# Streaming encoder layer on one core: the instruction order taken from a timeline simulation in place of the scheduler's usual machine model

## Chip, cores and metric

One NeuronCore of a Trainium2 chip runs the whole program in one launch. The metric is the device time of one execution in microseconds (us); lower is better. Engines are called PE (TensorE; PEld are its weight loads), DVE (VectorE), ACT (ScalarE), POOL (GpSimd) and SP (SyncE, which issues nearly all DMA transfers).

## The reference

One layer of a hybrid encoder is applied to two groups of rows that share all weights: 512 prompt rows and 64 sample rows of width 1024, in float32. Cut to what matters:

```
xn   = rmsnorm(x);  proj = xn @ w_in                      # 1024 x 3592
oa   = rmsnorm(gated_delta_rule(silu(conv(proj[q,k,v])))) * silu(z)   # 4 heads of 128
ob   = rmsnorm(softmax(q1 k1) v - lam * softmax(q2 k2) v)             # 4 heads of 128
h    = x + [oa, ob] @ w_out
h    = h + softmax(rmsnorm(h) @ w_mem_q  mem_k) mem_v @ w_mem_o       # 4 heads of 256
h    = h + relu(rmsnorm(h) @ w_ff1)**2 @ w_ff2                        # 1024 x 4096 x 1024
y    = rmsnorm(h)
```

The gated delta rule runs over blocks; within a block it needs the inverse of a triangular matrix, and from block to block it carries a 128 x 128 state for each head. The memory's keys and values (256 rows) are projected from a memory input for the prompt and read from a cache for the sample. Keys, values, states and convolution rows are outputs as well.

## The kernel before, in words

Rows and weights stay in float32, but the large products are made in three matmuls: each operand is split into a high part (a rounded copy, made on ACT) and a low part (the difference, made on DVE), and high x high, high x low and low x high are added up in PSUM. `weights` (L165) loads eight 128 x 128 blocks of a weight matrix into a `raw` tile (three buffers) and `split_weights` (L155) splits it into `wh` and `wl` (two buffers each). `project` (L169) multiplies it with all 576 columns in two halves, on one of three `pr` banks of PSUM, and an `evac` function carries the result away. `mm` (L106) and `tr` (L111) record every matmul and every transpose, so all of PE's rows in the profile bear L107 or L113; the tile's name tells which product it is (`pr` projections, `g` and `gs` small products of the delta rule and the attention, `ba` transposes and sums, later also products of the feed-forward part).

The stages follow each other in the code like this, though the engines overlap them:

- start (L365 to L429): rows are loaded, normed and turned, and the first three blocks of `w_in` are projected. This stage stands in `in_order()` (L52), which ties each engine's instructions to the order in which they are written.
- the rest of the q, k, v projections with the convolution (L440 to L463), about 35 to 105 us in the profile.
- the gated delta rule: `gdn_prep` (L653) makes, for each of four prompt chunks of 128 rows and one sample chunk, the gates and the triangular inverse, which it doubles level by level (five levels, L755 to L773, each a transpose and a product, a copy to SBUF, a second product, and a subtraction on DVE); `gdn_scan` (L811) then carries the state from chunk to chunk. Its square roots are powers on POOL (`rpow`, L207). The preparation of the next chunk, the scan of this one and the projections of z (`project_z`, L640) are independent and can be mixed.
- differential attention: `diff_project` (L946) makes q, k, v of a head, `diff_head` (L996) its scores, softmax and output for five row tiles.
- memory keys and values (L1080 to L1115), the output projection, memory attention (L1190 to L1249), with their projections.
- the feed-forward part: `ff1_pair` (L1380) makes two row blocks of the first product by seven products of sums of quarters, and `weights2`/`project` make the second product of the group before.
- the tail: last block, final norm, transposes back, stores.

What decides the order. The code is written as straight Python; every instruction is recorded with its tiles, and the order of each engine's queue is made when the `TileContext` closes. A list scheduler then steps a model of the machine. Each recorded instruction has a priority, the place where it stands in the code. Whenever an engine of the model can take an instruction, the scheduler gives it, among those whose inputs the model has finished and whose tile has a free buffer, the one with the highest priority. The buffer of a tile is chosen at the same time. The result is a fixed queue for every engine, SP and its transfers included, with semaphore waits between them. On the chip each queue runs in that order, whatever the real durations are. The scheduler's usual model is a core simulator that prices each instruction for its engine.

The code bends this order in four ways: `in_order()` (L52) for the start; `tc.high_priority()` around the splits of weights (L160, L1313, L1368), so that they come ahead of other ready work on ACT and DVE; `tc.keep_in_program_order` for single transfers, sums and transposes, most of them in the tail (`pin=True`); and `tc.issue_after(...)` (L467, L475, L599, L920, L940, L1561), which keeps early-ready work behind a named instruction of the same engine. These are edges that any order must keep.

Compiler passes after the scheduler put in the semaphore waits and the loads of ACT's function tables (Silu and Exp lie in different tables).

## Time and profile before

| | |
|---|---|
| runs | 987.23 us median of 3 (987.15 to 987.32) |
| the profiled execution | 987.2 us, of which the span from the first to the last instruction is 985.5 us |
| granted PE clock, mean | 0.997 |
| read from HBM, written | 79.93 MB, 9.75 MB |

The profile is one execution with every instruction's start and end on its engine. A row of instructions gives the line of the code, the engine, the operation, the tile written and the tiles read, the shape, the count, then busy time in us, the mean in ns, the idle time of the engine just before, and after an arrow the instruction that ended that idle time. A row of a timeline gives start and length in us. Ends of matmuls are modelled: the matmuls overlap in a pipeline, so that the busy time of PE is the time with at least one in it.

The chain of work that ended last, followed back from the end, runs over PE for 83% of the span, DVE for 4%, "issue" for 3%, and POOL, DMA and ACT for 2% each.

### The profile page before, as it was taken

The numbers are of one execution on the slowest core, as the hardware profiler recorded it, in microseconds if no ns is written. First come the engines' busy times: TensorE is split into PE (matmuls) and PEld (weight loads), VectorE is DVE, ScalarE is ACT, GpSimd is POOL, SyncE is SP. The second block draws the span as 40 slices with busy tenths as digits, with TensorE's granted clock in tenths as the row PEclk, the third lists the DMA queues.
The fourth block names the chain that finished last, engine by engine and source line by source line (L and its number), as shares of the span: only waits on it lengthen the run. The fifth ranks groups of instructions, "written<-read, shape, count | busy, mean of one in ns | idle before, by whom it ended". The sixth has DMA issues, their size and how long they took to land.

```text
span 985.5 us, 16923 instructions
## 1 busy us (share of the span) xinstructions
PE 968.5 (98%) x6403; PEld 891.2 (90%) x6403; DVE 699.7 (71%) x1570; ACT 530.1 (54%) x1194; POOL 58.8 (6%) x127
## 2 busy tenths in 40 slices
PE   9999999999999999999999999999999999999996
PEld 7989899898888878999999999999999999999996
DVE  6666787877676676666557977657867779978674
ACT  7545575344656665444445657665544445555444
POOL 3341011101000000000000000000000000000000
PEclk9999999999999999999999999999999999999998
DMA  7432340103222647333111414222222223223202
GB/s 212 129 119 65 90 138 23 43 23 103 81 68 68 203 131 227 95 94 99 44 44 58 127 54 127 86 86 86 86 87 86 86 86 86 86 86 86 65 23 96
DMA packets 121714, 90.75 MB, mean 92 GB/s; under 512 B 5564, under 2 KB 112206, under 8 KB 121122
## 3 DMA queue, kind: packets, MB, share of 16 engines
q1 hardware_dynamic: 121266, 89.03, 30.9%
q8 instruction: 50, 0.82, 0.3%
q10 hardware_dynamic: 368, 0.66, 0.2%
q14 instruction: 30, 0.25, 0.1%
HBM read 79.93 MB, written 9.75 MB: 91 GB/s over the span
## 4 chain that ended last, share of the span: by engine, by line
PE 83%; DVE 4%; issue 3%; POOL 2%; DMA 2%; ACT 2%; POOLq 0%; ACTq 0%; SPq 0%; DVEq 0%
PE pr L107 51%; PE g L107 12%; PE ba L107 10%; PE gs L107 6%; PE ba L113 3%; PE g L113 1%; POOL tg L208 1%; DMA r<-in_w_ff_dram 1%; DVE p L457 1%; DVE wl L162 0%; DMA grow<-gdram 0%; DMA raw<-in_w_ff_dram 0%; POOL X L607 0%; POOL X L608 0%; DVE on L809 0%
## 5 line engine op out<-in xcount | busy, mean ns | idle before, releaser
L107 PE MATMUL pr<-u,wh 128*128 128x320 f32 (+2 forms) x1240 | 328.7, 343 | 1.3 <-DVE p L323 1.2
L107 PEld LDWEIGHTS pr<-u,wh 128*128 128x128 f32 x1240 | 212.3, 188 | 18.0 <-DVE p L323 1.8
L107 PE MATMUL pr<-u,wl 128*128 128x256 f32 (+1 forms) x816 | 226.7, 302 | 0.0
L107 PEld LDWEIGHTS pr<-u,wl 128*128 128x128 f32 x816 | 149.9, 189 | 2.7 <-DVE wl L388 0.2
L162 DVE TENSOR_TENSOR wl<-raw,wh 128x1024 fp32r<-128x1024 f32 x65 | 79.4, 1223 | 41.3 <-ACT wh L161 41.0
L161 ACT CAST wh<-raw 128x1024 fp32r<-128x1024 f32 x65 | 68.1, 1048 | 65.7 <-PE pr L107 50.5
L107 PE MATMUL pr<-u,w2h 128*128 128x320 f32 (+1 forms) x384 | 98.5, 340 | 0.0
L1369 ACT CAST w2h<-r 128x512 fp32r<-128x512 f32 x56 | 34.7, 620 | 87.9 <-PE pr L107 85.3
L107 PE MATMUL pr<-f,w2h 128*128 128x320 f32 (+1 forms) x288 | 74.3, 340 | 0.1
L107 PEld LDWEIGHTS pr<-u,w2h 128*128 128x128 f32 x384 | 65.0, 188 | 4.5 <-ACT u L1452 0.3
L107 PE MATMUL pr<-u,w2l 128*128 128x256 f32 (+1 forms) x256 | 65.1, 295 | 0.0
L1454 DVE TENSOR_TENSOR u<-u,pr 128x256 f32<-128x256 f32 x96 | 42.3, 448 | 16.9 <-PE pr L107 16.2
L107 PE MATMUL ba<-u,wl 128*128 128x288 f32 x360 | 53.0, 296 | 0.4 <-ACT keep L1405 0.4
L107 PEld LDWEIGHTS pr<-f,w2h 128*128 128x128 f32 x288 | 48.7, 188 | 4.0 <-issue 1.1
L107 PEld LDWEIGHTS ba<-u,wl 128*128 128x128 f32 x360 | 49.2, 188 | 1.2 <-ACT keep L1405 1.1
L107 PE MATMUL pr<-f,w2l 128*128 128x256 f32 (+1 forms) x192 | 48.8, 295 | 0.0
L107 PEld LDWEIGHTS pr<-u,w2l 128*128 128x128 f32 x256 | 46.9, 188 | 1.5
L208 POOL TENSOR_TENSOR tiny<-tiny,nhalf 128x1 f32<-128x1 f32 (+4 forms) x10 | 8.7, 870 | 631.6 <-DVE tiny L1522 529.8
L1370 DVE TENSOR_TENSOR w2l<-r,w2h 128x512 fp32r<-128x512 f32 x56 | 38.5, 688 | 10.7 <-ACT w2h L1369 10.4
L107 PE MATMUL pr<-wh,u 128*128 128x512 f32 x128 | 41.4, 401 | 0.0
L1414 ACT ACTIVATE c<-c 128x288 f32<-128x288 f32 x48 | 20.6, 443 | 29.5 <-DVE c L1413 29.5
L107 PEld LDWEIGHTS pr<-f,w2l 128*128 128x128 f32 x192 | 35.2, 188 | 1.2
(514 smaller groups left out, 2025.1 us busy)
## 6 DMA issues: line engine op xcount, KB each, us to landing
raw<-in_w_ff_dram SPq DMA_DIRECT2D x36, 512.0 KB
raw<-in_w_in_dram SPq DMA_DIRECT2D x28, 512.0 KB
r<-in_w_ff_dram SPq DMA_DIRECT2D x56, 256.0 KB
raw<-in_w_mem_k_dram SPq DMA_DIRECT2D x8, 512.0 KB
raw<-in_w_mem_v_dram SPq DMA_DIRECT2D x8, 512.0 KB
raw<-in_w_out_dram SPq DMA_DIRECT2D x8, 512.0 KB
raw<-in_w_mem_q_dram SPq DMA_DIRECT2D x8, 512.0 KB
raw<-in_w_mem_o_dram SPq DMA_DIRECT2D x8, 512.0 KB
```

What stands on the lines that cost most here:

```text
L107: i = nc.tensor.matmul(out, lhsT, rhs, start=start, stop=stop, skip_group_check=skip_group_check)
L113: i = nc.tensor.transpose(out, in_, ident[:n, :n])
L161: A.copy(wh, raw)
L162: V.tensor_tensor(wl, raw, wh.bitcast(F32), ALU.subtract)
L208: G.tensor_tensor(out, in_, bc(nhalf[: in_.shape[0], 0:1], list(in_.shape)), ALU.pow)
L457: V.scalar_tensor_tensor(yv[:, :n], cb[:, i : i + n], cwt[:, m, i : i + 1], yv[:, :n], ALU.mult, ALU.add)
L1369: A.copy(wh, src)
L1370: V.tensor_tensor(wl, src, wh.bitcast(F32), ALU.subtract)
L1414: A.activation(c, c, AF.Relu)
L1454: V.tensor_tensor(am, am, b, ALU.add)
```

## The change

The scheduler steps another model of the machine: a simulation of the occupancy over time of each device in the core (sequencers, engines, PE's weight loader and array, DMA queues), with time for decoding, for waiting in an engine's queue, for the landing of a matmul's result and for semaphores to spread. It takes every function table of ACT as loaded. The list scheduler, the priorities, the tiles with their numbers of buffers, the edges that the code adds and all instructions recorded are those of before; which instruction is found ready at which moment, and so the order of each queue and the choice among buffers, comes from the other model.

```diff
@@ -1616,7 +1616,7 @@
-    with _tile.TileContext(nc) as tc:
+    with _tile.TileContext(nc, schedule_with_timeline_sim=True) as tc:
         hybrid_layer_kernel(tc, *args)
     r = _run(nc, [arrays], core_ids=[0])
```

## The prediction

> **What bounds the kernel now.** I read the page's head first, then the table by stretches of the span, then the waits of TensorE, and last the order of work around the longest of those waits. The page's head:
>
> ```profile
> span 985.5 us, 16923 instructions
> PE 968.5 (98%) x6403; PEld 891.2 (90%) x6403; DVE 699.7 (71%) x1570; ACT 530.1 (54%) x1194; POOL 58.8 (6%) x127
> ```
>
> The profiled execution took 987.2 us: a span of 985.5 and 1.7 around it. The median of the runs shown is 987.23, so a sum made against this execution holds for the runs. TensorE (PE) is busy for 968.5 us, so 985.5 - 968.5 = 17.0 us of it are visibly idle. Where those 17 us lie is in the stretches (columns: length, then busy time and instructions of PE, PEld, DVE, ACT and POOL, granted clock, DMA share, GB/s):
>
> ```profile
> 0.00:20.00 20.00, 18.35 (x97) 14.06 (x98) 10.93 (x14) 15.00 (x26) 9.11 (x23) 1.00 0.69 200
> 20.00:100.00 80.00, 78.72 (x514) 73.55 (x513) 53.74 (x94) 43.06 (x86) 25.36 (x75) 1.00 0.39 112
> 100.00:200.00 100.00, 97.44 (x726) 89.99 (x725) 81.45 (x228) 55.70 (x118) 11.87 (x14) 1.00 0.26 72
> 200.00:300.00 100.00, 98.20 (x666) 85.70 (x665) 71.39 (x221) 51.77 (x156) 5.79 (x9) 1.00 0.27 73
> 300.00:372.00 72.00, 71.03 (x402) 57.80 (x401) 49.13 (x133) 45.67 (x131) 3.95 (x5) 1.00 0.44 140
> 372.00:390.00 18.00, 18.00 (x81) 14.93 (x80) 10.92 (x12) 9.01 (x12) 0.00 (x0) 1.00 0.72 217
> 390.00:590.00 200.00, 200.00 (x1296) 185.68 (x1295) 136.50 (x325) 100.47 (x226) 1.17 (x1) 1.00 0.27 79
> 590.00:960.00 370.00, 369.15 (x2504) 352.25 (x2503) 275.59 (x530) 198.22 (x426) 0.00 (x0) 1.00 0.29 84
> 960.00:985.50 25.50, 17.64 (x134) 17.21 (x132) 10.09 (x20) 11.16 (x21) 1.55 (x2) 0.88 0.27 93
> ```
>
> The two ends hold 1.65 + 7.86 = 9.5 us of the idle time. The start is written out by hand and the last 8 us are norms, copies and stores that follow the last matmul, so a new order has little hold on either. From 390 to 960 us PE idles 0.85 us in 570. What an order can win visibly is in 20 to 372 us: 1.28 + 2.56 + 1.80 + 0.97 = 6.6 us. In 100 to 372 us (gated delta rule and differential attention), chains of small matmuls, each step waiting for DVE or ACT, are interleaved with the large projections that fill their waits.
>
> A second reading allows more. A matmul's record lasts longer than its share of the pipeline, so short waits hide inside "busy". Weight loads (PEld) show them better: from 590 to 960 us PEld is busy 352.25/370 = 95% of the time, from 20 to 100 us 73.55/80 = 92%, and from 100 to 372 us only 233.49/272 = 86%. At 92% the same loads would take 233.49/0.92 = 254 us, 18 us less. I take 18 us as the most that a perfect order wins in this stage, a rough estimate, since the mix of shapes differs.
>
> The Trainium skill ("Perfetto Trace Analysis", section "Identifying the Most-Contended Engine") says that matmul busy time is a poor measure of distance to the roofline and that weight-load busy time is a good one. By that rule the headroom is up to 985.5 - 891.2 = 94 us, not 17, which speaks for the gain below; no row here shows an order that reaches it.
>
> **The change part by part.** One keyword changes which machine model the scheduler steps while it orders the instructions and hands out buffers. No instruction is added or removed by it, apart from semaphore waits and table loads that the compiler places afterwards. PE's 6403 matmuls stay, and so do the edges that the kernel pins (start, tail, the blocks behind the keys) and the raised priority of the weight splits. So the sum is the old time plus changes in waiting.
>
> *Stages 20 to 100 and 372 to 960.* Here PE always has ready matmuls in excess; with ready work in priority order, any machine model gives nearly the same PE order. I cost them at 0. The cover is the splitting of the next weights by ACT and DVE ahead of time; its price if it goes stands at the second rival.
>
> *Stage 100 to 372.* Counting in the code, a "hop" (a group of small matmuls that waits for another engine, which then waits for it) occurs about 200 times: 25 doubling levels of the triangular inverse by 2, some 45 in the rest of gdn_prep, 24 in the scans, 20 attention tiles by 3, and some 22 transposes of projections. The levels can be checked: 4 chunks x 5 levels x 2 transposes, and 5 x 1 for the sample, make the 45 in the first row here:
>
> ```profile
> L113 PE MATMUL g<-ident,Y 128*128 128x128 f32 x45 | 9.3, 279 | 1.8 <-DVE tg L713 1.3 <-DVE Dt L772 0.4
> L107 PE MATMUL gs<-u,aT 128*128 128x128 f32 x96 | 15.1, 286 | 0.8 <-DVE on L809 0.8
> ```
>
> An engine runs its queue in order. When a hop's input comes later than the scheduler thought, everything behind it waits; when it comes earlier, the hop is late by the fillers ahead of it. The waits that PE shows in this stage:
>
> ```profile
> PE g L113 <- DVE tg L713: 1.3, 1, 1.3
> PE pr L107 <- DVE wl L162: 0.8, 1, 0.8
> PE gs L107 <- DVE on L809: 0.8, 1, 0.8
> PE g L113 <- DVE KQ L709: 0.5, 1, 0.5
> PE gs L113 <- DVE on L809: 0.5, 1, 0.5
> PE ba L107 <- DVE gg L548: 0.5, 1, 0.5
> PE g L113 <- DVE Dt L772: 0.4, 1, 0.4
> PE g L107 <- DVE At L705: 0.4, 1, 0.4
> ```
>
> Eight waits, 5.2 us, 0.65 us each: one hop in 25. How one comes about is seen in the timeline at 194 us:
>
> ```profile
> 193.86 1.64 POOL L208 TENSOR_TENSOR tg<-tg,nhalf 128x8 f32<-128x8 f32 x1 [3.15 <-DVE tg L688]
> ...
> 195.53 0.16 DVE L712 TENSOR_TENSOR tg<-tg,tg 128x4 f32<-128x4 f32 x1 [1.31 <-POOL tg L208]
> 195.61 0.42 DVE L772 TENSOR_TENSOR Dt<-Dt,g 128x256 f32<-128x256 f32 x1
> ...
> 196.18 0.41 PE L113 MATMUL g<-ident,Y 128*128 128x128 f32 x2 [1.25 <-DVE tg L713]
> ```
>
> The power on POOL (queue of its own) took 1.64 us; DVE had L712 next, which needs it, and stood still for 1.31 us; the subtraction L772 of another chunk was ready behind it; PE waited 1.25 us for that subtraction's successor. One small instruction put ahead of another on DVE costs PE 1.25 us. The new order deals these positions again, about 200 times, on PE, DVE, ACT and POOL.
>
> The trace doesn't show the new rate of misses, so I bound it. Below: none, which wins the 5.2 us (18 with the hidden ones). Above: one hop in three, 67 x 0.65 = 43, less the 5.2 that are there, +38 us. I take one in eight: 25 x 0.65 = 16.3, less 5.2, +11 us. It lies nearer the row shown (one in 25) than the upper end, and above that row because the old rate is already low: DVE is 81% busy from 100 to 200 us, so nearly every change of its order delays something that another engine wants. What would be late next if the waits went is the PE stream itself.
>
> *Table loads on ACT.* The timeline model counts every activation table as loaded, so it sees no cost in alternating Silu, of the z projections, with Exp, of the gates. The trace has 11 such loads; one pair:
>
> ```profile
> 108.44 1.28 ACT L525 ACT_TABLE_LOAD   x1
> 109.73 0.22 ACT L525 ACTIVATE t<-t 128x20 f32<-128x20 f32 x1
> 109.97 1.28 ACT L647 ACT_TABLE_LOAD   x1
> ```
>
> The likely change is a few loads, 1.28 us each on an engine that is 44% idle in that stretch: 0 on the path. Bounds: the Silu loads gone (-4 us of ACT time) or 11 more, 14 us, all on the path. The Trainium skill ("ScalarE: Activation LUTs", section "What ACT_TABLE_LOAD costs") puts about 1.38 us of draining beside each 1.28 us; 11 more would then be 29 us. The trace disagrees: the activation starts 1.29 us after the load.
>
> *SyncE.* Its queue is in order as well, and a load that waits for a free buffer holds up those behind it:
>
> ```profile
> SPq L157 <- DVE wl L162: 116.4, 25, 18.6
> SPq L1475 <- DVE u L1478: 18.9, 1, 18.9
> ```
>
> Waits of up to 18.9 us stand there now, covered by loads made ahead: 0.
>
> **Sum:** 987.2 + 11 + 0 + 0 + 0 = 998 us.
>
> **The rivals.**
> *Faster.* The timeline model times each device more closely, so hops are placed where the chip is ready for them and the waits shrink. For: 18 us of loss in 100 to 372 us. Against: visible waits are only 5.2 us there. Half of the 18 gives 987.2 - 9 = 978 us, all of it 969. It decides the sign once fewer than one hop in 25 misses.
> *Slower by late weights.* If SyncE gets a non-urgent transfer ahead of an urgent load, the load comes up to 18.9 us late. The lead is about two split tiles; the dense run
>
> ```profile
> 65.78 36.17 PE pr L107 x224
> ```
>
> gives 161 ns a matmul, 6.5 us for a projection's 40, so a lead of 13 us and 6 us lost per such event. Two of them, with the hops' 11 and half of the 11 table loads (7), make 987.2 + 30 = 1017 us. For: the long SyncE waits. Against: DMA engines are only 27 to 29% busy after 390 us.
> *The same.* The new order could be nearly the old one: priorities and pins are unchanged. 985.5 to 989 us. Against: 200 hops interleaved matmul by matmul leave little chance of equal sequences.
> *The order doesn't change at all* would be 987.2 and is part of that case.
>
> **How the numbers follow.** Slower by missed hops, 998 us (own range 989 to 1012): 0.42. Slower by late weights or table loads, 1005 to 1040: 0.14. The same: 0.08. Faster, 969 to 985: 0.36. A measurement of this kernel can tell about 0.2%, 2 us, from no change, so faster 0.36, same 0.08, slower 0.56. The range 972 to 1022 leaves out the lower part of the faster case (0.09) and the upper part of the second (0.07).
>
> **What would show it.** The PE waits by line in 100 to 372 us should grow from eight to about 25, on L113 and L107 of gdn_prep, gdn_scan and diff_head, and PE's busy time there fall by about 11 us of a longer stretch; PEld's total should stay near 891. From 390 to 960 us PE should stay over 99% busy. For the faster case PEld's share in that stage must rise above 86%. Table loads should number 8 to 14; 20 or more would speak for the second rival, as would waits of PE for wl, w2l or a raw tile. I am wrong in kind if time is lost in the dense stages, at the start or in the tail, or if the granted clock drops inside the span: the tail's 0.88 shows that it falls where PE idles 7.9 us of 25.5.

## The result, and the profile after

The changed kernel takes **1051.34 us** (median of 4 runs, 1049.72 to 1052.41), beside 987.28 us (987.15 to 987.56) for the kernel before on the same chip: **1.0647** times as long, 95% interval 1.0629 to 1.0666. The direction was forecast, the size was not: the sum said 998 and its range ended at 1022.

First the head of the page of the changed kernel (instructions, busy times, the granted clock in 40 slices, the chain that ended last):

```profile
span 1048.0 us, 16897 instructions
...
PE 986.7 (94%) x6403; PEld 908.1 (87%) x6403; DVE 702.3 (67%) x1570; ACT 540.0 (52%) x1198; POOL 60.8 (6%) x127
...
PEclk9899999999978999999999999999999999999999
...
PE 83%; DVE 6%; ACT 4%; issue 3%; DMA 2%; SPq 1%; POOL 0%; POOLq 0%; DVEq 0%; ACTq 0%
```

The same 6403 matmuls keep PE busy for 986.7 instead of 968.5 us, 18.2 more, and the span has 1048.0 - 986.7 = 61.3 us without a matmul instead of 17.0, 44.3 more. Together these are the whole difference, 62.5 us. That equal matmuls are busy for longer is in part the clock's doing: three slices show it below 0.9, and in the records of the clock it stands at half for 51.9 us of the span, instead of 6.3 (at the very end) before. How large that part can be is worked out behind the experiments.

Next, both spans cut at the same places of the work (columns: length, then busy time and instructions of PE, PEld, DVE, ACT and POOL, granted clock, DMA share, GB/s). The eight stretches are the start; the rest of the convolution; up to the inverse of the first chunk; up to the end of the last scan; up to the end of the attention; what is left of the memory's keys and values; the output projection and memory attention; the feed-forward part with the tail. Before:

```profile
0.00:37.00 37.00, 35.35 (x218) 30.57 (x219) 21.97 (x32) 22.98 (x41) 11.80 (x34) 1.00 0.66 179
37.00:106.00 69.00, 67.72 (x433) 62.07 (x431) 47.96 (x84) 37.79 (x75) 23.03 (x64) 1.00 0.36 103
106.00:160.00 54.00, 53.05 (x384) 49.11 (x385) 43.88 (x132) 36.48 (x79) 5.89 (x7) 1.00 0.30 89
160.00:244.00 84.00, 81.38 (x635) 74.70 (x634) 63.59 (x175) 35.51 (x85) 9.41 (x11) 1.00 0.20 52
244.00:358.00 114.00, 113.05 (x672) 94.34 (x671) 79.79 (x253) 69.71 (x221) 4.78 (x7) 1.00 0.35 108
358.00:394.00 36.00, 35.19 (x168) 28.79 (x166) 23.53 (x28) 20.42 (x30) 1.17 (x1) 1.00 0.67 201
394.00:584.00 190.00, 190.00 (x1229) 176.34 (x1228) 127.95 (x312) 92.86 (x211) 1.17 (x1) 1.00 0.27 78
584.00:985.00 401.00, 392.78 (x2679) 375.24 (x2677) 291.07 (x559) 214.32 (x456) 1.55 (x2) 0.99 0.28 83
```

After:

```profile
0.00:47.00 47.00, 38.92 (x221) 33.79 (x222) 23.28 (x34) 23.93 (x42) 13.41 (x34) 0.89 0.54 145
47.00:113.00 66.00, 66.00 (x428) 61.55 (x426) 46.47 (x83) 36.88 (x73) 23.71 (x65) 1.00 0.35 105
113.00:206.00 93.00, 89.89 (x614) 83.32 (x612) 58.06 (x152) 52.27 (x99) 6.14 (x8) 1.00 0.32 86
206.00:287.00 81.00, 62.26 (x467) 54.22 (x465) 53.26 (x151) 27.18 (x67) 9.08 (x10) 0.96 0.07 21
287.00:443.00 156.00, 137.32 (x705) 111.30 (x704) 90.57 (x265) 77.34 (x237) 4.54 (x7) 0.91 0.33 107
443.00:459.00 16.00, 15.30 (x79) 12.39 (x78) 14.06 (x20) 11.88 (x20) 1.17 (x1) 1.00 0.52 160
459.00:653.00 194.00, 190.42 (x1223) 177.26 (x1222) 128.73 (x309) 91.48 (x209) 1.17 (x1) 0.99 0.26 76
653.00:1048.00 395.00, 386.64 (x2679) 374.32 (x2677) 287.87 (x562) 219.02 (x458) 1.55 (x2) 0.99 0.28 85
```

Read them pair by pair. The start loses 10 us at a clock of 0.89. The stretch up to the first chunk's inverse takes 93 instead of 54 us, but PE is busy in it: it issues 614 matmuls there instead of 384. The scans then have 467 instead of 635 matmuls and 19 us of idle PE; the attention takes 156 instead of 114 us, with 19 us idle and a clock of 0.91; the stretch after it is shorter by 20 us, since its matmuls have been issued already. The feed-forward part gained: its 2679 matmuls are busy for 386.64 instead of 392.78 us.

**The start.** ACT in the changed kernel (start and length in us, idle time before in brackets), and from PE's waits (us in total, times, longest) the longest one, which comes of it, the next, and the only one for a split weight block behind the start:

```profile
16.96 0.59 ACT L288 CAST u<-g 128x512 fp32r<-128x512 f32 x1 [0.54 <-PE g L113]
24.88 0.20 ACT L515 ACTIVATE tiny<-dtb 128x4 f32<-128x4 f32 x1 [7.33 <-DMA dtb<-in_a_log_dram]
24.99 0.57 ACT L288 CAST u<-ba 128x512 fp32r<-128x512 f32 x1
```

```profile
PE pr L107 <- ACT kd L410: 6.7, 1, 6.7
PE g L113 <- DVE Dt L772: 4.8, 7, 1.8
...
PE pr L107 <- DVE wl L162: 0.2, 1, 0.2
```

L515 is the exponential of `a_log`, four numbers that are first needed for the gates, behind the convolution. It is written behind the start that `in_order()` fixes, but that order only ties its own instructions to each other; the new order put this one between two of them, and ACT stood in front of its load for 7.33 us with the turned rows ready behind it.

**The delta rule.** DVE's last two steps of a level in the changed kernel (L771 makes `Y`, the input of the next level; L772 is the subtraction), and PE's queue up to the next level's transposes, which read `Y`:

```profile
179.68 0.29 DVE L771 TENSOR_TENSOR Y<-Dt,g 128x128 f32<-128x128 f32 x1
180.00 0.42 DVE L772 TENSOR_TENSOR Dt<-Dt,g 128x256 f32<-128x256 f32 x1
```

```profile
182.25 0.31 PE L107 MATMUL pr<-u,wl 128*128 128x320 f32 x1
182.40 0.46 PE L107 MATMUL pr<-u,wh 128*128 128x320 f32 x2
182.69 0.31 PE L107 MATMUL pr<-u,wl 128*128 128x320 f32 x1
182.84 0.38 PE L113 MATMUL g<-ident,Y 128*128 128x128 f32 x2
```

Both steps are done at 180.42; the transposes come 2.4 us later, behind a run of projection matmuls that has lasted since 178.32. (Two chunks take these steps 0.7 us apart, and the rows don't say which is which; 2.4 us is the least.) Fifty us on, no projection is left and the chain of small products is bare:

```profile
230.71 0.44 PE L113 MATMUL g<-ident,Y 128*128 128x128 f32 x2 [2.11 <-DVE Y L751]
230.98 0.62 PE L107 MATMUL g<-Dt,B 128*128 128x128 f32 x4
231.45 1.00 PE L113 MATMUL g<-ident,u 128*128 128x128 f32 x4
```

Counted in the order of the matmul queue, the five inverses end behind 737, 751, 838, 884 and 927 projection matmuls before, and behind 956, 956, 956, 956 and 1036 after: 219 more stand ahead of the first inverse, and none is left between the first and the fourth.

### The profile page after: what moved, and what is told of

The parts are those of the page before. It is cut to its first block, busy times and chain, and to the rows that moved or that the text cites. A ratio compares the mean times of both kernels' runs of the same rounds, so it can differ in the third digit from the quotient of the medians.

```text
span 1048.0 us, 16897 instructions
## 1 busy us (share of the span) xinstructions
PE 986.7 (94%) x6403; PEld 908.1 (87%) x6403; DVE 702.3 (67%) x1570; ACT 540.0 (52%) x1198; POOL 60.8 (6%) x127
## 4 chain that ended last, share of the span: by engine, by line
PE 83%; DVE 6%; ACT 4%; issue 3%; DMA 2%; SPq 1%; POOL 0%; POOLq 0%; DVEq 0%; ACTq 0%
PE pr L107 52%; PE g L107 11%; PE ba L107 10%; PE gs L107 6%; PE ba L113 2%; PE g L113 2%; DMA raw<-in_w_in_dram 1%; DMA grow<-gdram 1%; ACT p L1022 0%; DVE wl L162 0%; DMA dtb<-in_a_log_dram 0%; DVE u L202 0%; SPq L129 0%; DVE At L705 0%; DVE Y L764 0%
## 5 line engine op out<-in xcount | busy, mean ns | idle before, releaser
L107 PE MATMUL pr<-u,wh 128*128 128x320 f32 (+2 forms) x1240 | 322.5, 341 | 2.1 <-ACT qz L957 0.7
L107 PE MATMUL pr<-u,wl 128*128 128x256 f32 (+1 forms) x816 | 223.3, 298 | 0.0
L107 PE MATMUL pr<-u,w2l 128*128 128x320 f32 (+1 forms) x256 | 65.4, 295 | 0.0
L107 PEld LDWEIGHTS pr<-f,w2h 128*128 128x128 f32 x288 | 49.2, 188 | 2.5
L107 PE MATMUL g<-u,qz 128*128 128x256 f32 (+4 forms) x96 | 30.8, 439 | 4.1 <-ACT p L1022 3.4
```

Source lines behind the costliest of these rows:

```text
L107: i = nc.tensor.matmul(out, lhsT, rhs, start=start, stop=stop, skip_group_check=skip_group_check)
```

## The experiments

Every stage below is measured between the same events in the trace (first output of the convolution, last one, inverse of the first chunk copied, last scan's output, last output of the attention, first sum of the output projection, first product of the feed-forward part, end), so that kernels can be set beside each other. The recorded expectations call the third of these events the second inverse, or that of the second chunk; the trace says otherwise: in the kernel before it ends at 159.5 us, the first scan reads this inverse at 163.4, and the next chunk's is copied at 168.6. In the changed kernel the two copies end within 0.7 us of each other. Idle is time of the span without a matmul, half the time at a granted clock of 0.5. All in us:

| kernel | median | start | conv. | to 1st inverse | scans | attention | memory k, v | proj., mem. att. | feed-fwd | idle | half |
|---|---|---|---|---|---|---|---|---|---|---|---|
| before | 987.3 | 37.4 | 68.5 | 53.7 | 84.9 | 113.9 | 35.8 | 189.5 | 401.9 | 17.0 | 6.3 |
| after | 1051.3 | 47.3 | 66.1 | 92.9 | 80.6 | 156.0 | 16.3 | 194.1 | 394.7 | 61.3 | 51.9 |
| ea_late | 1041.6 | 38.3 | 66.1 | 92.3 | 82.2 | 156.1 | 16.2 | 194.1 | 394.7 | 53.0 | 48.3 |
| pe_usual | 1021.9 | 49.2 | 66.0 | 61.1 | 92.5 | 124.5 | 35.1 | 191.6 | 401.7 | 43.7 | 30.1 |
| pe_timeline | 1076.6 | 37.7 | 67.4 | 99.4 | 86.6 | 168.8 | 15.6 | 197.6 | 403.6 | 81.6 | 72.1 |
| rest_usual | 1137.7 | 37.1 | 74.0 | 73.0 | 113.0 | 143.4 | 36.5 | 215.8 | 442.7 | 123 | 68 |
| pe_act_usual | 1007.0 | 37.6 | 67.8 | 59.7 | 90.6 | 124.0 | 35.1 | 191.5 | 400.2 | 31.2 | 15.0 |
| pe_dve_usual | 1005.2 | 37.3 | 67.4 | 55.1 | 85.1 | 118.6 | 35.8 | 191.7 | 411.2 | 33.8 | 4.9 |
| two_queues | 989.8 | 37.8 | 67.4 | 55.3 | 85.1 | 118.8 | 35.8 | 192.3 | 395.5 | 23.2 | 7.0 |
| del10 | 1064.7 | 37.4 | 68.4 | 63.0 | 100.3 | 164.3 | 37.4 | 189.5 | 401.2 | 74.0 | 37.7 |
| del20 | 1109.1 | 37.5 | 68.4 | 70.5 | 104.9 | 195.5 | 38.3 | 189.5 | 402.0 | 99.6 | 78.8 |
| adv10 | 1087.1 | 38.2 | 66.9 | 93.3 | 85.9 | 196.4 | 16.5 | 195.0 | 394.7 | 79.2 | 88.6 |
| early9 | 1029.1 | 37.8 | 68.5 | 91.2 | 85.1 | 119.5 | 30.5 | 189.6 | 404.4 | 42.7 | 25.5 |
| early29 | 1045.5 | 37.9 | 68.5 | 91.2 | 83.7 | 154.9 | 14.7 | 189.5 | 401.8 | 50.6 | 36.8 |
| hold9 | 1031.9 | 38.0 | 66.1 | 70.5 | 94.5 | 153.6 | 16.8 | 196.1 | 394.7 | 49.7 | 31.7 |
| hold29 | 1042.4 | 37.8 | 66.0 | 70.3 | 96.4 | 152.5 | 26.8 | 197.4 | 394.7 | 54.9 | 45.0 |
| usual_to_out | 985.8 | 37.8 | 68.4 | 53.6 | 84.9 | 113.9 | 35.9 | 195.0 | 394.7 | 20.4 | 10.4 |
| usual_to_ff | 982.7 | 37.9 | 68.5 | 53.7 | 84.9 | 113.9 | 35.9 | 191.1 | 394.8 | 17.2 | 6.3 |

My theory was: the start loses 10 us by L515, and the delta rule and the attention lose the rest because small products stand behind projection matmuls, which are used up early and are missing later. The rival: the place of work in the matmul queue is harmless, and the orders of the other queues cost.

**ea_late**: the one instruction is put behind the start on its engine.

```diff
-    A.activation(ea, dtb[:, 1, :], AF.Exp)
+    with tc.issue_after(opened[mybir.EngineType.Activation]):
+        A.activation(ea, dtb[:, 1, :], AF.Exp)
```

> Timeline model, with one edge more: the exponential of a_log (L515) may not be issued on ACT before the hand-ordered start has ended. Theory (a small instruction that waits for its load stands in the middle of the start on ACT): the 7.3 us wait of ACT at 17 us and the 6.7 us wait of PE go, the clock is not halved from 23 to 33 us, and the time falls by 8 to 10 us, to about 1041. Rival (the start is late because SyncE brings weights after the small loads): the first convolution still ends at 47 us and the time stays at 1050.

Measured 1041.63 us (1039.84 to 1041.84), ratio 1.0542 [1.0526, 1.0558]: 9.7 us less than the changed kernel. ACT's queue no longer stops at 17.6 us:

```profile
17.64 0.59 ACT L288 CAST u<-g 128x512 fp32r<-128x512 f32 x1 [0.39 <-PE g L113]
18.12 0.59 ACT L288 CAST u<-ba 128x512 fp32r<-128x512 f32 x1
```

The start is settled: one instruction of 0.20 us costs 9.7.

**Which queue holds the loss.** The next kernels record the program twice: once with one model, to learn its order, and once with the other model, with edges that tie the named engines' queues to the order learnt.

```diff
+        with _tile.TileContext(nc, schedule_with_timeline_sim=timeline) as tc:
+            hybrid_layer_kernel(tc, *args)
+            traced = list(nc.cur_bb.bb.instructions)
+            if follow is not None:
+                keep_order(tc, traced, follow)
...
+    def keep_order(tc, traced, follow):
+        last = {}
+        for n in follow:
+            i = traced[n]
+            if i.engine not in PINNED:
+                continue
+            if i.engine in last:
+                tc.add_manual_dep(
+                    i, last[i.engine].name,
+                    _mybir.DependencyInfo(_mybir.DependencyClass.NoSync, _mybir.DependencyReason.DATA),
+                    reason="keep_order",
+                )
+            last[i.engine] = i
```

*pe_usual*: flag on, PE in the usual order.

> Timeline model, but PE's queue is tied to the order that the usual model gives; ACT, DVE, POOL and SyncE are ordered by the timeline model. L515 stands early on ACT as in the changed kernel. Theory (PE's order is the cause in the delta rule and the attention: long runs of projections ahead of small products whose inputs are ready): only the start's loss of about 10 us is left, 995 to 1000 us. Rival (the orders of DVE, ACT and SyncE carry the loss): above 1030 us.

Measured 1021.86 us, ratio 1.0348 [1.0332, 1.0363]: 29 us of the 64 go, fewer than the theory expected and more than the rival. *pe_timeline* is the converse, usual model and PE in the timeline's order:

> The converse: the usual model orders ACT, DVE, POOL and SyncE, and PE's queue is tied to the order of the changed kernel. L515 stands late, as before. Theory (PE's order): 1037 to 1043 us, that is the changed kernel's time less the start's 10 us, with the projections used up by 206 us again. Rival (the other engines' orders): 990 to 1000 us.

Measured 1076.63 us (1071.55 to 1079.9), ratio 1.0896 [1.0860, 1.0931], worse than the changed kernel itself. *rest_usual* has the flag on and every queue but PE's in the usual order:

> Timeline model, with ACT, DVE, POOL and SyncE tied to the usual orders; only PE is ordered by the timeline model. If the model itself puts small products behind projections that are already in PE's queue, PE's waits and idle time stay and it takes 1005 to 1040 us, though the other engines' fixed orders hold the projections back in part; if PE's order in the changed kernel merely follows from the others' orders, it takes 987 to 992 us.

Measured 1137.74 us, ratio 1.1522 [1.1503, 1.1541], the worst of this set, with 40 us lost in the feed-forward part alone (442.7 against 401.9), where neither pure order loses anything. These two misses taught that queues of two models don't fit together, so that tying one engine can add a cost of its own. The expectations had left that out. Ties of two engines then went as follows. *pe_act_usual*:

> Flag on, the matmul queue and ACT's queue tied to the usual order, DVE, POOL and SP by the timeline model. With the matmul queue alone tied it took 1021.9, which leaves 34 us over the kernel before, 10 to 12 of them at the start. Theory (ACT's order carries the start and what else is left): 995 to 1000. Rival one (only the start is ACT's, the rest is DVE's): about 1010. Rival two (queues of two models don't fit together whichever they are): 1022 or more.

Measured 1007.01 us (1006.28 to 1008.3), ratio 1.0201 [1.0187, 1.0215], near the first rival's 1010. Beside pe_usual only the start changes much (37.6 instead of 49.2); the delta rule and the attention stay as they were. *pe_dve_usual* (with L515 behind the start):

> Flag on, the matmul queue and DVE's queue tied to the usual order, ACT, POOL and SP by the timeline model, and the exponential of a_log behind the hand-ordered start. Theory (ACT's order carries what is left): the start's 10 us go and no more, about 1012. Rival one (the rest is DVE's): 995 to 1000. Rival two (queues of two models don't fit): 1022 or more.

Measured 1005.23 us (1004.2 to 1007.54), ratio 1.0189 [1.0173, 1.0204], between the forecasts of the theory and the first rival. Here the delta rule is back at its old times (55.1 and 85.1) and the attention at 118.6; instead the feed-forward part takes 411.2, a misfit as in rest_usual. Tying the two queues only up to the feed-forward part should take that away. *two_queues*:

```diff
+            queue = [n for n in follow if traced[n].engine == engine]
+            tied = max((p for p, n in enumerate(queue) if n < CUT[-1]), default=-1) + 1
+            for p in range(1, len(queue)):
+                tc.add_manual_dep(
+                    traced[queue[p]], traced[queue[min(p, tied) - 1]].name,
+                    _mybir.DependencyInfo(_mybir.DependencyClass.NoSync, _mybir.DependencyReason.DATA),
+                    reason="keep_order",
+                )
```

> Flag on; the matmul queue and DVE's queue are tied to the usual order up to the feed-forward part, the exponential of a_log stands behind the hand-ordered start, and all else (ACT, POOL, SP, and every queue in the feed-forward part) is ordered by the timeline model. Theory (the matmul and vector queues and that one instruction hold the whole loss; the 10 us that the feed-forward part lost when only two of its queues were tied were a seam of two models): stages up to the feed-forward part about 591 as there, the rest 394.8: 986 to 989. Rival (ACT's order costs as well, 5 us or more behind the start): 993 or more.

Measured 989.79 us (987.95 to 991.44), ratio 1.0018 [1.0009, 1.0028], just above the expected 986 to 989 and 3 us under the rival's 993. The total flatters, since it holds the feed-forward part's gain of 6.4 us: the stages ahead of it take 592.5 us, against 583.7 before and 653.3 after. So the orders of PE and DVE there, and L515, hold 61 of the 70 us that these stages lost. What is left shows as 5 us in the attention and 3 in the projection and memory attention (118.8 and 192.3 us against 113.9 and 189.5).

**Shifting all products.** To see what in PE's order costs, every product of the delta rule and the attention on a `g` or `gs` bank was moved past 10 or 20 projection matmuls, with the other four queues unchanged: later in the kernel before (*del10*, *del20*), earlier in the changed kernel with L515 late (*adv10*).

```diff
+                while k - 1 > floor and kind[queue[k - 1]] != "small" and passed < abs(SHIFT):
+                    k -= 1
+                    passed += kind[queue[k]] == "long"
+                queue.insert(k, queue.pop(p))
```

> The kernel before, its five queues in their own order, but on the matmul queue each product of the delta rule and of the differential attention (those that write the g and gs banks) is put behind up to 10 projection matmuls more, as far as the data allow; the four other queues are untouched. Theory (products that stand behind projection matmuls lengthen every hop of the chains, use up the projections early and leave the chains bare): 10 matmuls are about 2.3 us a hop, half of what the changed kernel put there; the stage up to the last inverse of the second chunk takes 65 to 80 us instead of 53.7, the attention 120 to 135 instead of 113.9, the whole 1003 to 1020. Rival (the place in the matmul queue is not what costs, the other engines' orders are): 985 to 992.

> As the last with up to 20 matmuls more, about what the changed kernel has between two hops. Theory: about twice the loss of 10, 1020 to 1045, with the matmul clock halved in stretches behind bare chains. Rival: 985 to 992.

> The changed kernel with the exponential of a_log behind the hand-ordered start (1041.6 as measured), its five queues in their own order, but on the matmul queue each product of the delta rule and of the differential attention is put ahead of up to 10 of the projection matmuls before it, as far as the data allow; the four other queues are untouched. Theory: 2.3 us less a hop, the stage up to the last inverse of the second chunk takes 65 to 78 us instead of 92.3; the whole 1012 to 1028. Rival (the other engines' orders hold the chains back, so a product that comes earlier in the matmul queue only waits there): 1036 or more.

Measured: del10 1064.68 us, ratio 1.0778 [1.0762, 1.0794]; del20 1109.14, 1.1233 [1.1214, 1.1252]; adv10 1087.12, 1.1000 [1.0973, 1.1028]. All three forecasts of the theory missed: the first two fell far short of the loss, the last had the wrong sign (1087.12 fits the rival's open range). The experiment can't tell the theories apart. If each product moves by 10, as many matmuls as before lie between two of them; so the stretch up to the first chunk's inverse grew by only 9 us in del10 and changed by 1 in adv10. The attention took most of the loss (164 and 196 us), probably because its transposes on the `ba` bank stayed where they were and the products lost their turn among them. The waits of PE in del10 and then in adv10 (us in total, times, longest):

```profile
PE ba L113 <- DVE p L1027: 18.9, 14, 2.8
PE ba L113 <- DVE ta L1020: 9.3, 6, 2.2
```

```profile
PE g L107 <- ACT p L1022: 16.3, 15, 2.1
PE gs L107 <- ACT aT L1034: 11.0, 15, 2.2
```

What they do show is how little room a finished order has: moving one kind of product past ten matmuls cost 77 us in one direction and 45 in the other.

**The count alone.** Better tests change how many projection matmuls stand ahead of a few places, with all else left to the scheduler. Nine places lie in the delta rule (the ends of five inverses and four scans), twenty in the attention (the first product of each block). *hold*: in the timeline order no projection matmul comes ahead of a place that it follows in the usual order. *early*: in the usual order no place comes ahead of the projection matmuls that the timeline puts before it. The edges of the two, *hold* first:

```diff
+            if n in ANCHORS[-ANCHORED:]:
+                anchor = traced[n].name
+            elif anchor and outs[n].startswith("pr_"):
+                tc.add_manual_dep(traced[n], anchor, NO_SYNC, reason="hold")
...
+            if n in ANCHORS[-ANCHORED:] and behind:
+                tc.add_manual_dep(traced[n], behind, NO_SYNC, reason="hold")
+            elif outs[n].startswith("pr_"):
+                behind = traced[n].name
```

> The converse in the kernel before: the usual order, but none of the nine places comes ahead of the projection matmuls that the timeline order puts before it; the counts ahead of the five inverses go from 737, 751, 838, 884, 927 to 956, 956, 956, 956, 1036. All else is left to the usual scheduler. Theory: the stage up to the second inverse takes about 90 us instead of 53.7, the chains behind it run bare, idle matmul time rises by 15 to 30 us and the clock halves in stretches, the whole 1005 to 1025. Rival: 985 to 992.

Measured 1029.06 us (1026.71 to 1031.37), ratio 1.0424 [1.0401, 1.0446], a little over the theory's range and far from the rival's 992. The stretch up to the first chunk's inverse takes 91.2 instead of 53.7 us, and the idle time of the scans rises from 2.6 to 19.5 us, as in the changed kernel; the attention, where only the first head's projections are touched, takes 119.5 us, 5.6 more than before.

> As early9 (1029.1), with the same twenty places in the attention: none comes ahead of the projection matmuls that the timeline order puts before it. All else is left to the usual scheduler. Theory: the attention takes 135 to 155 us instead of 119.5, the whole 1040 to 1060. Rival: 1024 to 1034.

Measured 1045.48 us (1043.87 to 1048.78), ratio 1.0603 [1.0584, 1.0623]. The stretches of early29 from the end of the convolution to the end of the attention:

```profile
106.00:198.00 92.00, 90.91 (x628) 84.01 (x627) 57.54 (x152) 46.73 (x96) 6.20 (x8) 1.00 0.31 84
198.00:281.00 83.00, 63.71 (x472) 55.28 (x471) 54.57 (x161) 28.93 (x74) 9.10 (x10) 0.96 0.10 30
281.00:436.00 155.00, 136.90 (x688) 107.31 (x687) 87.08 (x254) 75.40 (x225) 4.60 (x7) 0.92 0.32 104
```

Set these beside the third to fifth rows of the changed kernel: 92, 83 and 155 us against 93, 81 and 156, with PE busy for the same times within 1.5 us and the same drop of the clock. Twenty-nine edges in the usual order, on the count of projection matmuls alone, make the changed kernel's loss behind the start. That the projections are issued ahead of these places is therefore **enough** to cause it. (An edge does two things at once: it uses up projections early and holds the chain back until they are through; the two were not separated.) Is it also needed? The converse:

> Flag on, the exponential of a_log behind the hand-ordered start (1041.6 as measured). Nine places are picked in the delta rule: the transposes that end the inverse of each of the five chunks, and those that end each of the four scans. A projection matmul that follows such a place in the usual order may not be issued ahead of it. All else is left to the timeline model. The count of projection matmuls ahead of the five inverses goes from 956, 956, 956, 956, 1036 to 737, 751, 838, 863, 927; from the second head of the attention on nothing changes. Theory (projections used up early leave the later chains bare): the stage up to the second inverse 55 to 65 us instead of 92.3, idle matmul time in the scans under 10 us instead of 17.9, the whole 1008 to 1024. Rival (the count is harmless, other parts of the queues' orders cost): 1035 or more.

Measured 1031.92 us (1030.2 to 1033.08), ratio 1.0449 [1.0433, 1.0464]: 9.7 us less than ea_late, not the 18 to 34 that the theory expected, and not the rival's 1035 either. The stretch up to the first chunk's inverse falls from 92.3 to 70.5 us, the idle time in the scans from 17.9 to 11.7.

> As hold9 (1031.9), with twenty places more: the first product of each of the four heads' five blocks of queries. No projection matmul that follows such a place in the usual order may be issued ahead of it. The counts of projection matmuls ahead of the attention's first, sixth, eleventh and sixteenth block go from 927, 1060, 1156, 1256 to about 927, 996, 1056, 1131. All else is left to the timeline model. Theory (the same mechanism holds in the attention): the attention takes 118 to 132 us instead of 153.6, the whole 998 to 1012. Rival (in the attention it is the other engines' orders): 1025 or more.

Measured 1042.35 us (1036.22 to 1043.7), ratio 1.0548 [1.0516, 1.0581]: the attention stays at 152.5 us and the whole takes 10 us more than hold9, so here the rival's number came. A likely reason can be seen in PE's queue in the attention of hold29 and, below it, of the kernel before:

```profile
347.44 0.69 PE L107 MATMUL pr<-u,wh 128*128 128x320 f32 x3
347.97 0.76 PE L107 MATMUL g<-u,qz 128*128 128x256 f32 x4
348.57 0.89 PE L107 MATMUL gs<-u,aT 128*128 128x128 f32 x6
349.29 0.60 PE L113 MATMUL ba<-ident,p 128*128 128x128 f32 x4
349.73 0.38 PE L113 MATMUL ba<-ident,u 128*128 128x128 f32 x2
```

```profile
294.01 0.39 PE L107 MATMUL pr<-u,wh 128*128 128x512 f32 x1
294.28 0.71 PE L107 MATMUL gs<-u,aT 128*128 128x128 f32 x4
294.74 0.36 PE L107 MATMUL pr<-u,wl 128*128 128x256 f32 x1
294.95 0.39 PE L107 MATMUL pr<-u,wh 128*128 128x512 f32 x1
```

In the timeline order small products stand in a bunch (scores of two blocks, outputs, transposes), with the projections in a bunch ahead of them; in the usual order the two alternate more finely. Over the attention, hold29's matmul queue has the small ones in 34 runs of up to 40, with 9 projection matmuls (median) between two runs; the kernel before has 59 runs of at most 17, with 4 between. The edges fixed how many projections were left for each block, not that they were spread between its products. pe_usual, in which they are, has the attention at 124.5 us. So undoing the count alone wins back only a part (9.7 us in hold9), and the spreading is the likely rest; no run sets the spreading alone.

**A better version.** Since most of what the new order gains lies in the feed-forward part, *usual_to_ff* ties all five queues to the usual order up to there (the edit is that of two_queues, with all engines and without the edge on L515), and *usual_to_out* up to the output projection.

> All five queues are tied to the usual order up to the last instruction that is written ahead of the feed-forward part; what follows on each engine is ordered by the timeline model. Theory (the loss sits in the start and in the chains of the delta rule and the attention, where the order decides what is ready; the dense end loses nothing): the stages up to the feed-forward part take their 585 us of before, the rest its 394.7 instead of 401.9 us, so about 980. Rival one (the 7 us that the feed-forward stage had less in the changed kernel were only work done earlier): 987. Rival two (the timeline order costs everywhere, also where the matmul queue is never empty): above 992.

> As the last, but the queues are tied only up to the projection behind the attention; that projection, the attention over memory and the feed-forward part are ordered by the timeline model. Theory: the stage of projection and memory attention took 194.1 us in the changed kernel and 189.5 before, with 3.6 us of idle matmul time and 3.4 us at half clock, because hops stand behind queued matmuls there too: about 985 (980 + 4.6). Rival (those 4.6 us were handed on from the stages ahead): 980.

Measured 982.70 us (982.11 to 983.05), ratio **0.9952** [0.9940, 0.9965], and 985.78 (984.17 to 987.19), 0.9986 [0.9977, 0.9995]. The first is faster than both kernels, by 0.5% beside the kernel before. It lies between the theory's 980 and the first rival's 987: the feed-forward part gains the 7 us, and the projection and memory attention ahead of it lose 1.6 (191.1). Its feed-forward stretch has the changed kernel's 386 us of busy PE:

```profile
586.00:981.00 395.00, 386.30 (x2677) 374.03 (x2675) 287.73 (x561) 218.50 (x457) 1.55 (x2) 0.99 0.28 85
```

The second keeps the changed kernel's projection and memory attention, which cost it 195.0 instead of 189.5 us: the new order loses there as well, if little. The 6 us in the feed-forward part are waits too short to show as idle time. From start to start, matmuls of one shape keep the same pace before and after (133 ns for the commonest, 128x288). But before, 67 starts come more than 20 ns later than is usual behind the shape ahead, 7.7 us in sum, and after only 13, 1.6 us in sum. Most of these delays lie inside a record of the matmul ahead, so that PE counts as busy.

## Why the prediction was right in direction and wrong in size

*The step that failed: "Stage 100 to 372", with its +11 us.* It priced the new order as single missed hops, one in eight, 0.65 us each. Two things were wrong with it. The rate: from 113 to 443 us PE of the changed kernel waits visibly 55 times, 39.5 us in all, 0.72 us each; so one wait was priced rightly and their number was twice the 25 assumed. Less the 5.2 us that were there, this is +34 where +11 was said. And the picture: it took each miss as a loss of its own, at its place. In fact the first stretch, where products come 2.4 us late behind projections, loses hardly any PE time (3.1 us idle), because the projections are useful work. The bill comes later, when the same projections are missing: 18.7 us idle in the scans, 18.7 in the attention. early9 and early29 show this chain of cause from the usual order. The upper bound, +38 us for one hop in three, held for the waits alone; what the sum had no term for is that PE also stays busy for longer. From the end of the convolution to the end of the memory's keys and values the changed kernel takes 57.5 us more: 36 idle, and 21.6 busy with the same matmuls.

*"Stages 20 to 100 and 372 to 960. I cost them at 0"* and *"the start is written out by hand"*. The start lost 9.7 us by ea_late: a fixed order ties only what stands in it, and the reading overlooked that an instruction from outside can be queued between. The cover named there, ready work in excess, did hold behind the start: the convolution gained 2.4 us, projection and memory attention lost 4.6, the feed-forward part gained 7.2, together a gain of 5.0 where 0 was said.

*The clock.* The prediction named a drop of the granted clock inside the span, and time lost at the start, as signs that it is wrong in kind, and both came. It put no price on the clock, although the end of the kernel before showed a drop. The clock stood at half for 45.6 us more. In the stretches at half clock PE was busy for 37.5 us, and if every matmul in them took twice its time, the clock makes at most 37.5 / 2 = 18.8 us of busy time. Records of single 128x128 products last 421 ns there and 275 at full clock. This is not all: in early29 PE is busy for 23.0 us more than before, with 26.9 busy us at half clock, which can make 13.5. Another part can be estimated. In a run of 128x128 products the next one starts 111 ns after the last (median); where PE runs dry, the whole record of the last one shows, 0.16 us more. From the end of the convolution to the end of the memory's keys and values PE runs dry 74 times instead of 15, which makes some 9 us, part of them at half clock. PEld's total rose too, to 908.1 where "near 891" was said.

*Table loads.* 15 instead of 11, outside the 8 to 14 forecast and under the 20 that would have spoken for the second rival. What they cost by themselves was not tried. But early29 has 11 loads, as the kernel before, and loses as much behind the start as the changed kernel, so the four more are not needed for the loss.

*Rival "slower by late weights".* Behind the start PE waits once for a split weight block, the 0.2 us for `wl` shown above, and two_queues leaves SP's order alone and takes 989.8 us: this rival fell.

*Rival "faster".* Its 18 us of hidden waits lie in 100 to 372 us, and nothing was won there. What the new order won lies in the feed-forward part, where the prediction saw nothing to win: PE was visibly idle for 0.85 us in 370, yet the same matmuls became 6 us shorter. The prediction's own second reading, that short waits hide inside "busy", was right, but it put the room into another stage. Visible idle time is not all the room that there is.

What stays open is why the timeline model issues the projections so early. The queue in front of the transposes at 182.84 suggests that it hands PE long runs of ready matmuls before the next small product is ready in the model; the runs show only the effect of its choices. The sign was forecast from late hops, and waits did make the larger part of the loss; but they came by another route than the one pictured, and the start's 9.7 us and the 21.6 us of longer busy time were in no term of the sum.

## What to carry to other kernels

When long independent work fills the waits of short chains, ask of a new order not only whether each step finds its place but how much of the filler is left at each link of the chain: filler that is issued early looks busy and is missed 50 us later, and then the clock is lost too. A scheduler's result is a set of queues that belong together; taking PE's queue from one order and the rest from the other cost more here in two of three cases (1077 and 1138 us; 1022 in the third) than either whole order, so compare stage by stage, and mix at a point where all queues are cut. And an order fixed by hand holds only against its own members: look for cheap instructions with a late input that can be slipped in between.

## What the runs showed of the hardware

The granted clock changes in steps: all stretches at half clock inside the changed kernel last 3.41, 10.24 or 20.48 us, that is 1, 3 or 6 times 3.41. In the changed kernel, a stretch in the middle of the span:

```profile
300.00:303.00 3.00, 1.40 (x8) 0.85 (x6) 0.90 (x4) 0.49 (x2) 0.00 (x0) 1.00 0.60 178
303.00:324.00 21.00, 14.96 (x46) 11.04 (x47) 8.54 (x35) 6.61 (x26) 0.00 (x0) 0.51 0.08 25
324.00:340.00 16.00, 14.44 (x87) 11.31 (x86) 8.57 (x27) 8.95 (x31) 0.16 (x1) 1.00 0.15 49
```

Three us in which PE was busy for 1.40 are followed by 20.5 us at half clock, although PE was busy for 71% of them (14.96 of 21). Cut into windows of 3.41 us that are aligned with the changes, the trace of the changed kernel has half clock after a full-clock window when PE was visibly busy for 48% of that window or less (eight windows, 0 to 0.48; the lowest two that kept full clock had 0.47 and 0.48), and full clock comes back only after a window at half clock with 90% or more (seven windows; six of 0.50 to 0.94 did not bring it back). These shares are no sharp thresholds: in rest_usual a window busy for 67% (from 306.5 us) was followed by half clock, and in pe_usual one that was busy throughout (from 128.2 us) did not bring full clock back. So a chain that is bare for a few us is paid twice: once by its idle time, and then by slow matmuls until a window is nearly full. The Trainium skill ("TensorE: Matmul & The Clock Gate", section "What's actually happening") states windows of about 3.4 us, which the trace bears out, and names an idle window as what takes the clock down; here a window that was busy for up to 48% did it, and the measurement decides.
